# An eighth accumulation bank for C22 in a seven-product matmul kernel, side products moved to four banks between seven-product pairs

## The chip, the cores and the metric

The kernel runs on one core of a Trainium2 chip. The metric is the device time of one execution in microseconds (us); a median over several runs is given. The engines are PE (TensorE, matmuls), DVE (VectorE), ACT (ScalarE), POOL (GpSimd) and SP (SyncE); POOL and SP only issue DMAs here, apart from a few small powers on POOL.

## The reference

A trunk of two layers over 256 tokens of width 4096, all in float32. The two large products of a layer, into 11,264 columns and back from 4096 to 4096, make nearly all of the work.

```
for l in range(DEPTH):                       # DEPTH = 2
    h = rmsnorm(x, norm_w[l])
    proj = h @ w_in[l]                       # (256 x 4096) @ (4096 x 11264)
    aq, ak, av, ag, rq, rk, rv, rg = split(proj)
    a_out = silu(ag) * gqa_attention(rope(norm(aq)), rope(norm(ak)), av)     # 16 heads, 4 for keys
    r_out = silu(rg) * rmsnorm(bidirectional_retention(rope(rq), rope(rk), rv))   # 8 heads
    x = x + concat([a_out, r_out]) @ w_out[l]   # (256 x 4096) @ (4096 x 4096)
return rmsnorm(x, final_norm)
```

## The kernel before

**Blocks.** Each projection is cut into blocks of 2 x 512 columns: 11 blocks for `w_in`, 4 for `w_out`, so that the two layers have four *stages* with 11, 4, 11 and 4 blocks. One block computes a 2 x 2 array of outputs C11, C12, C21, C22 (two halves of 128 tokens by two halves of 512 columns). The 32 row tiles of the contraction are taken as 16 *pairs* (`NP`), each a 2 x 2 by 2 x 2 product.

**Precision.** A float32 operand is split into a rounded high part and the rest as a low part (`whi`, `wlo` for weights, `x8h`, `x8l`, `x7h`, `x7l` for activations). One *product* is three matmuls of 128 x 128 by 128 x 512: high x high and low x high of the operand with the weights' high part (L1472), and high x the weights' low part (L1482). In the very first block pairs 0 and 1 (`NATIVE`) are taken unsplit in one slower matmul each (L1466).

**Seven or eight products.** A pair costs eight products. Pairs in the seven-product set (`SEVEN`, with pair 10 added in stages 1, 2 and 3 by `MORE`) use Winograd's form with seven: sums of weights and sums of activations are formed first (`xf` in `split_pair`, `wsum` in `Weights.begin`), and the seven products go to seven banks M1 to M7 of the accumulator memory (each bank holds 128 x 512 numbers). So that eight-product pairs can share these seven banks, they don't accumulate C22 in a bank of its own: one bank (M3) takes a *difference operand*, x of the one half minus x of the other, and M5 takes both halves' rest:

```
EIGHT_PRODUCTS: ("M3", 1, 2, PAGE_A, 1), ("M5", 1, 1, PAGE_A, 1), ("M4", 0, 1, PAGE_A, 0), ("M2", 0, 0, PAGE_A, 0), ...
```

The second index 2 is the difference, which `split_pair` makes for each eight-product pair (`x3`, shown as `x` in the profile), and which the first stage makes later, in `third`. Only the first block of all (`PLAIN`) has an eighth bank, which has the tag `ps`, and there `PLAIN_PRODUCTS` is used.

**Pages.** The weights of a pair come in two pages of 128 x 1024 (A, B); a seven-product pair has two more for the sums (T, U). A page is loaded by SP into one of 5 raw buffers, ACT rounds it (`whi`), DVE subtracts (`wlo`), and PE uses it; 5 such pages are in the ring. For some pages (`FAR_PAIRS`, `FAR_OUT`) the low part is made without DVE: ACT writes minus the high part (`flo`), and POOL adds the weights to it by a DMA that reads them a second time (L521).

**Between blocks.** As soon as a bank has its last product, `combine` adds it into the block's output pages `ca`, `cb` (DVE, at M1 ACT). All products of the last pair are sorted by bank (`LAST_ORDER`), so that the banks come free one after the other before the next block starts with them.

**Side products.** Attention and retention need 576 small matmuls of their own (L988 to L990). They share the eighth bank, `ps`: `take_bank` waits until it is free, `free_bank` returns it. Their steps are *tasks* and *lanes* (Python generators) that a planner (`tick`, `advance`, `running`) places between the products: it keeps a modelled time of PE, DVE and ACT, lets a task step run only where the next pages still come in time (`Weights.room`, with `STEP_V`, `STEP_S`, `MARGIN`), and counts *pages* of working memory (`PAGES` = 9). The order that it finds at build time is the order of the instructions on the chip.

**End.** In the last block, products of bank M4 with the pairs in `DELAYED` (5) come last, so that the other half's output is finished beside them (`last_combine`).

Of the kernel before, what the change touches and what calls it, by code (L numbers as in the profile page):

```python
# [17 lines left out]
P = 128  # L18
# [17 lines left out]
PAGES = 9  # L36
# [5 lines left out]
STEP_V = 0.8  # L42
STEP_S = 1.5

V_FIXED = 0.1
S_FIXED = 0.12

MM = {512: 0.2268, 256: 0.1177}
PASS = 0.3

LANDING = 9.5
STORE = 7.0
FETCH = 13.0
FAR_LANDING = 11.0
MARGIN = 0.8

RUSH = 0.5
# [3 lines left out]
ADD_AHEAD = 0.5  # L61

NEED = {"ak": 4, "ag": 4, "rk": 5, "rg": 4}

PE_REST = 1.5

TIGHT_A = 2
TIGHT_B = 9

AT_ONCE = 2  # L70
# [19 lines left out]
PLAIN = 1  # L90

DEFER = (0,)

FAR_PAIRS = (2, 8, 11, 14)

FAR_OUT = (5, 14)
# [17 lines left out]
def constants():  # L114
# [60 lines left out]

SEVENS = [tuple(sorted(SEVEN + MORE)) if _s in MORE_IN else SEVEN for _s in range(2 * DEPTH)]
EVER = sorted(SEVEN + MORE)
EIGHTS = [_p for _p in range(NP) if _p not in EVER]

GROUPS = [[tuple(range(_a, _b)) for _a, _b in zip(_s, _s[1:] + (NP,))] for _s in SEVENS]  # L180


def pages_of(group, first=False):

    order, one = [], group[:1]
    rest = group[1:]
# [12 lines left out]
def is_far(stage, p, k):  # L199

    return k == PAGE_B and p in (FAR_OUT if stage % 2 else FAR_PAIRS)


def slots_of(group, stage, first=False, plain=False):

    for _p, _k in pages_of(group, first):
        if _p in SEVENS[stage] and not (first and _p in NATIVE):
            yield [(_b, _p, (ALL, _a), _k, _h) for _b, _a, _pg, _h in SEVEN_PRODUCTS if _pg == _k]
        else:
            eight = PLAIN_PRODUCTS if plain else EIGHT_PRODUCTS  # L210
            yield [(_b, _p, (_i, _a), _k, _h) for _b, _i, _a, _pg, _h in eight if _pg == _k]
# [3 lines left out]
LAST_ORDER = ("M3", "M5", "M4", "M2")  # L215
FINAL_ORDER = ("M5", "M2", "M3", "M4")
PLAIN_ORDER = ("M3", "M8", "M4", "M2")
# [7 lines left out]
TOGETHER = 3  # L225
# [3 lines left out]
TURNS = "02"  # L229

ABREAST = False
# [46 lines left out]
def hybrid_encoder(  # L278
# [136 lines left out]
    class Weights:  # L415


        def __init__(self):
            self.pages = []
            for l in range(DEPTH):  # L420
                for w, n in ((w_in, N_IN), (w_out, N_OUT2)):
                    for b in range(n):
                        stage = 2 * l + (w is w_out)
                        for g in GROUPS[stage]:
                            start = (l, b) == (0, 0) and w is w_in
                            for slot in slots_of(g, stage, start):
# [5 lines left out]
                                    start and (g in GROUPS[0][:2] or one.whole)  # L432
# [164 lines left out]
    def dead_room():  # L597

        if not rooms:
            e, o = len(EIGHTS), len(EVER)  # L600
            kinds = {
                "x3": ("x3", e, [P, 2, 2, P], "p k s t -> p (k s t)"),
# [5 lines left out]
            for p in range(NP):  # L608
                if p not in EIGHTS:
                    rooms.extend(kinds[v] for v in ("x7h", "x7l"))  # L610
                else:
                    rooms.extend(kinds[v] for v in ("x3", "x8h", "x8l")[: 3 if p in EIGHTS[2:] and p not in DELAYED else 1])
# [20 lines left out]
    def split_pair(p, v, whole, stage):  # L633
# [39 lines left out]
        else:  # L673
            if p in EIGHTS:
                hi = t(ap, [P, 2, SEQ], "x8h", len(EIGHTS), F32R)
                lo = t(ap, [P, 2, SEQ], "x8l", len(EIGHTS), F32R)
                g = t(ap, [P, 2, 2, P], "x3", len(EIGHTS), F32R)
                g = [g[:, k] for k in range(2)]
            else:
                both = [t(ap, [P, 7, P], v, len(EVER), F32R) for v in ("x7h", "x7l")]  # L680
                hi, lo = (v[:, 0:4, :].rearrange("p (i m) t -> p i (m t)", m=MT) for v in both)
                g = [v[:, 4:6, :] for v in both]
            g4 = [tokens(v) for v in g]
# [10 lines left out]
            if stage in DEFER:  # L694
                thirds.append(Lane(None))
                thirds[-1].steps = third(p, hi, lo, g, thirds[-1])
                thirds[-1].pair, thirds[-1].at_work = p, False
            else:
# [8 lines left out]
        operand[p] = (hi, lo) if p in SEVENS[stage] else (hi, lo, g)  # L707
# [3 lines left out]
    def third(p, hi, lo, g, one):  # L711

        while held[0] + pledged() >= PAGES:
            yield
        one.at_work = True
        v = page([P, 2, 2, P], "x3f")
        d, e = v[:, 0], v[:, 1]
        for u, v in ((d, hi), (e, lo)):
            ve.tensor_sub(u, f32(v)[:, :, :P], f32(v)[:, :, P:])
        ve.tensor_add(d, d, e)  # L720
        yield
        ac.copy(g[0], d)
        yield
        ve.tensor_sub(g[1], d, f32(g[0]))
        drop()
        operand_at[p] = ve.until + PASS
        yield

    as_it_comes, thirds = {}, []

    def third_step():
        one = thirds[0]
        if not one.at_work and held[0] + pledged() >= PAGES:
            advance()
            return
        one.step()
        if one.done:
            thirds.pop(0)
# [92 lines left out]
    bank = [False, 0.0]  # L831
# [9 lines left out]
    def free_bank():  # L841
        bank[0], bank[1] = False, max(ve.until, ac.until) + BANK_REST

    class Lane:
        def __init__(self, steps, heavy=True, need=0, own=0, owner=None):
# [41 lines left out]
    def running():  # L887
# [3 lines left out]
        if rest and len(one) < AT_ONCE:  # L891
            need = held[0] + rest[0].need - rest[0].own + sum(max(0, w.need - w.own) for w in one)
            if need <= PAGES:
                one.append(rest[0])
# [946 lines left out]
```

## Time and profile before

| | |
|---|---|
| median of 3 runs | 2619.73 us (2616.75 to 2621.66) |
| profiled execution | 2620.23 us |
| its span, first to last instruction | 2618.4 us |
| granted clock of PE | 0.998 |
| DVE operations on `wlo<-wraw,whi` | 853, 929.5 us |
| ACT casts `whi<-wraw` | 853, 808.8 us |
| DMA moved | 660.34 MB, mean 252 GB/s |

The page gives the busy time of each engine, its share of the span and the number of instructions, then the clock granted to PE in 40 slices (9 is full), then the chain of work that ended last. In a row of a timeline the first number is the start and the second the duration of one, both in us; in a group the numbers behind the bar are busy us and mean ns of one, then the idle time before them and what ended it. A row of the waits has the total, the number of waits and the longest. A row of a window has its length, then busy us (and instructions) of PE, PEld (weight loads of PE), DVE, ACT and POOL, then the clock, the DMA share and GB/s.

### The profile page before, as it was taken

The page shows a single profiled execution, that of the slowest core. Times are in us where ns is not written, and L with a number is a line of the kernel's source. Part 1 is how long each engine was busy: PE and PEld are TensorE (multiplying, and loading weights), DVE is VectorE, ACT ScalarE, POOL GpSimd, SP SyncE. Part 2 cuts the span into 40 slices and gives each one's busy share as a digit, 9 for nine tenths or more (in the row PEclk, how much of TensorE's full clock was granted, in tenths as well). Part 3 has the DMA queues.
Part 4 walks back from the last instruction along what each step waited for, and adds up shares of the span by engine and source line. Part 5 has one row for each costly group of instructions (what it writes and reads, how often), then busy time and mean ns, then how long its engine had stood idle before and what let it go on. Part 6 is the DMA issues. An engine that isn't in the chain of part 4 may idle for free.

```text
span 2618.4 us, 34300 instructions
## 1 busy us (share of the span) xinstructions
PE 2595.2 (99%) x11596; PEld 2142.3 (82%) x11596; DVE 2257.9 (86%) x2786; ACT 1774.0 (68%) x2552; POOL 325.7 (12%) x464
## 2 busy tenths in 40 slices
PE   9999999999999999999999999999999999999998
PEld 7778888888888888888878888888888888788886
DVE  7898887888878899887998989988898798998787
ACT  8767676656655787555886767676566567876554
POOL 0012221201101100111111112221011011000000
PEclk9999999999999999999999999999999999999999
DMA  8888888878777776887788888878787777767785
GB/s 308 290 256 273 278 266 268 266 253 258 221 228 243 242 243 212 262 270 236 273 249 255 274 268 266 285 251 275 250 256 224 237 245 247 225 211 244 241 252 186
DMA packets 194497, 660.34 MB, mean 252 GB/s; under 512 B 23440, under 2 KB 30096, under 8 KB 194320
## 3 DMA queue, kind: packets, MB, share of 16 engines
q1 hardware_dynamic: 147760, 521.27, 57.0%
q0 software_dynamic: 46560, 136.87, 21.8%
q8 instruction: 91, 1.49, 0.2%
q14 instruction: 86, 0.70, 0.1%
HBM read 614.01 MB, written 44.04 MB: 251 GB/s over the span
## 4 chain that ended last, share of the span: by engine, by line
PE 92%; DMA 3%; DVE 2%; ACT 2%; issue 1%; SPq 0%; DVEq 0%; POOLq 0%; POOL 0%; ACTq 0%
PE M L1472 59%; PE M L1482 29%; DMA wraw<-in_w_in 2%; DVE wlo L263 1%; PE ps L989 1%; PE ps L988 1%; PE ps L990 1%; ACT whi L263 1%; DMA flo<-in_w_in 0%; PE M L1466 0%; DMA ca<-in_x 0%; DVE wsum L263 0%; ACT to L263 0%; PE ps L1472 0%; DMA fhi<-in_w_in 0%
## 5 line engine op out<-in xcount | busy, mean ns | idle before, releaser
L263 ACT CAST whi<-wraw 128x1024 fp32r<-128x1024 f32 (+1 forms) x853 | 808.8, 960 | 476.3 <-PE M L1472 284.1
L263 DVE TENSOR_TENSOR wlo<-wraw,whi 128x1024 fp32r<-128x1024 f32 (+1 forms) x853 | 929.5, 1107 | 155.5 <-ACT whi L263 146.6
L1472 PE MATMUL M<-whi,x8h 128*128 128x512 f32 x1467 | 572.6, 390 | 0.8 <-DVE ca L263 0.8
L1472 PE MATMUL M<-whi,x8l 128*128 128x512 f32 x1467 | 571.5, 390 | 0.0
L1482 PE MATMUL M<-wlo,x8h 128*128 128x512 f32 x1467 | 505.0, 389 | 0.0
L1472 PE MATMUL M<-whi,x7h 128*128 128x512 f32 x1262 | 491.6, 390 | 2.3 <-DVE cb L263 1.3
L1472 PE MATMUL M<-whi,x7l 128*128 128x512 f32 x1262 | 491.4, 389 | 0.0
L263 ACT CAST whi<-wsum 128x1024 fp32r<-128x1024 f32 x336 | 352.8, 1050 | 185.7 <-PE M L1472 130.2
L263 DVE TENSOR_TENSOR wlo<-wsum,whi 128x1024 fp32r<-128x1024 f32 x336 | 409.5, 1219 | 70.6 <-ACT whi L263 63.0
L1482 PE MATMUL M<-wlo,x7h 128*128 128x512 f32 x1262 | 414.1, 390 | 0.7 <-DVE wlo L263 0.2
L1472 PEld LDWEIGHTS M<-whi,x8h 128*128 128x128 f32 x1467 | 275.8, 188 | 60.7 <-DVE ca L263 3.2
L1472 PEld LDWEIGHTS M<-whi,x8l 128*128 128x128 f32 x1467 | 275.8, 188 | 57.2 <-issue 0.2
L1482 PEld LDWEIGHTS M<-wlo,x8h 128*128 128x128 f32 x1467 | 275.7, 188 | 57.1
L1472 PE MATMUL M<-whi,x 128*128 128x512 f32 x960 | 296.2, 390 | 1.1 <-ACT whi L263 1.1
L1482 PEld LDWEIGHTS M<-wlo,x7h 128*128 128x128 f32 x1262 | 236.6, 188 | 52.9 <-DVE wlo L263 3.9
L1472 PEld LDWEIGHTS M<-whi,x7h 128*128 128x128 f32 x1262 | 237.1, 188 | 51.3 <-DVE cb L263 1.6
L1472 PEld LDWEIGHTS M<-whi,x7l 128*128 128x128 f32 x1262 | 237.0, 188 | 48.2
L263 DVE TENSOR_TENSOR wsum<-wraw 128x1024 f32<-128x1024 f32 x168 | 204.2, 1216 | 29.4 <-DMA wraw<-in_w_in 26.1
L1472 PEld LDWEIGHTS M<-whi,x 128*128 128x128 f32 x960 | 180.1, 188 | 38.8 <-ACT whi L263 1.5
L1482 PE MATMUL M<-wlo,x 128*128 128x512 f32 x480 | 187.2, 390 | 0.4 <-DVE wlo L263 0.4
L521 POOL DMA_DIRECT2D flo<-in_w_in x87 | 79.4, 913 | 825.3 <-ACT flo L263 812.8
L263 ACT CAST fhi<-wraw 128x1024 fp32r<-128x1024 f32 (+1 forms) x103 | 107.9, 1048 | 88.8 <-PE M L1472 88.6
(298 smaller groups left out, 2873.5 us busy)
## 6 DMA issues: line engine op xcount, KB each, us to landing
wraw<-in_w_in SPq DMA_DIRECT2D x700, 512.0 KB, 5.0
wraw<-in_w_out SPq DMA_DIRECT2D x256, 512.0 KB, 4.6
flo<-in_w_in POOLq DMA_DIRECT2D x87, 512.0 KB, 7.9
full<-next_dram POOLq DMA_DIRECT2D x18, 512.0 KB, 8.2
p_dram<-room POOLq DMA_DIRECT2D x64, 128.0 KB, 4.7
pT<-p_dram POOLq DMA_DIRECT2D x16, 512.0 KB, 7.8
flo<-in_w_out POOLq DMA_DIRECT2D x15, 512.0 KB, 7.6
next_dram<-room POOLq DMA_DIRECT2D x40, 128.0 KB, 5.3
```

Of the source, the lines that this page charges most:

```text
L263: return call(out, *args, **kwargs)
L521: nc.gpsimd.dma_start(g.lo[h], g.src[0][:, h, :], accum_op=ALU.add)
L988: nc.tensor.matmul(out, a[0], b[0], start=start, stop=False)
L989: nc.tensor.matmul(out, a[0], b[1], start=False, stop=False)
L990: nc.tensor.matmul(out, a[1], b[0], start=False, stop=stop)
L1472: nc.tensor.matmul(acc[name], a[i], g.hi[h], start=m == first[name] and not i, stop=False)
L1482: nc.tensor.matmul(acc[name], a, g.lo[h], start=False, stop=m == final[name])
```

## The change

- An eighth bank, M8, takes C22 in all blocks. Eight-product pairs use the list that was `PLAIN_PRODUCTS`. The difference operand, its tile and `third` are gone.
- `SEVENS` names the seven-product pairs of each stage. Each stage has 5; pair 0 is in none, so a block opens and, past the last of them, closes with eight-product pairs, which don't use M1, M5, M6 and M7.
- Side products take any of these four banks (`SHARED`), in the *window* from the end of a block's last seven-product pair to the start of the next block's first. `take_bank`, `free_bank`, `near` and gates on tasks see to that. In the first block of an output projection (`hurried`) all side work has to be placed before the first seven-product pair.
- Attention's scores and values become two tasks; retention's weights are a gated lane. Tasks start in any order that fits (`startable`).
- `PAGES` is 13 instead of 9. The constants of the planner change, `TOGETHER` is 4 (so many products of a page are issued with their high parts first), and fewer pages are read twice (`FARS`).
- Four pairs instead of five are delayed at the end.

```diff
-PAGES = 9
+PAGES = 13
...
-STEP_V = 0.8
-STEP_S = 1.5
+STEP_V = 1.6
+STEP_S = 0.7
...
-SEVEN = (0, 3, 6, 9, 12)
-
-MORE = (10,)
-
-MORE_IN = (1, 2, 3)
-
-DELAYED = tuple([_p for _p in range(NP) if _p not in SEVEN + MORE][-5:])
+SEVENS = ((3, 5, 7, 9, 11), (5, 7, 9, 10, 11), (3, 5, 7, 9, 11), (5, 7, 10, 11, 12))
+
+EVER = sorted(set(_p for _s in SEVENS for _p in _s))
+EIGHTS = [_p for _p in range(NP) if _p not in EVER]
+
+DELAYED = tuple(EIGHTS[-4:])
...
-FAR_PAIRS = (2, 8, 11, 14)
-
-FAR_OUT = (5, 14)
+FARS = ((2, 12), (1, 8), (12,), (15,))
...
 EIGHT_PRODUCTS = [
-    ("M3", 1, 2, PAGE_A, 1),
-    ("M5", 1, 1, PAGE_A, 1),
-    ("M4", 0, 1, PAGE_A, 0),
-    ("M2", 0, 0, PAGE_A, 0),
-    ("M4", 1, 1, PAGE_B, 1),
-    ("M5", 0, 1, PAGE_B, 0),
-    ("M3", 0, 2, PAGE_B, 0),
-    ("M2", 1, 0, PAGE_B, 1),
-]
-
-PLAIN_PRODUCTS = [
     ("M3", 1, 0, PAGE_A, 1),
     ("M8", 1, 1, PAGE_A, 1),
...
+SHARED = ("M1", "M5", "M7", "M6")
...
-LAST_ORDER = ("M3", "M5", "M4", "M2")
-FINAL_ORDER = ("M5", "M2", "M3", "M4")
+LAST_ORDER = ("M3", "M8", "M4", "M2")
+FINAL_ORDER = ("M8", "M2", "M3", "M4")
...
-TOGETHER = 3
+TOGETHER = 4
...
-            if stage in DEFER:
-                thirds.append(Lane(None))
-                thirds[-1].steps = third(p, hi, lo, g, thirds[-1])
-                thirds[-1].pair, thirds[-1].at_work = p, False
-            else:
-                ve.tensor_sub(x0, x0, x1)
-                yield
-                ac.copy(g4[0], x0)
-                yield
-                ve.tensor_sub(g4[1], x0, f32(g4[0]))
...
     def take_bank():
 
-        while bank[0] or now.t < bank[1]:
-            yield
-        bank[0] = True
+        while not (window[1] and any(v <= now.t for v in spare.values())):
+            yield
+        name = min(spare, key=lambda v: spare[v])
+        del spare[name]
+        taken[name] = None
         yield "PE"
-        return t(pm, [P, NB], "ps")
+        taken[name] = t(pm, [P, NB], name)
+        return taken[name]
...
             if n == first[name]:
-                acc[name] = t(pm, [P, NB], "ps" if name == "M8" else name)
+                if name in SHARED:
+                    if name == SHARED[0] and hurried:
+                        while users:
+                            advance()
+                    window[1] = False
+                    while name in taken:
+                        advance()
+                    now.wait(spare.pop(name, 0.0))
+                acc[name] = t(pm, [P, NB], name)
...
         if bank == "M6":
             ve.tensor_add(cb[:, 0, :], ca[:, 0, :], acc["M6"])
             ve.tensor_add(ca[:, 1, :], cb[:, 0, :], acc["M7"])
-            if "M8" in acc:
-                combine("M5 and M6", acc, c)
+            ve.tensor_add(cb[:, 1, :], ca[:, 1, :], acc["M5"])
+            ve.tensor_add(cb[:, 0, :], cb[:, 0, :], acc["M5"])
+            for v in SHARED:
+                spare[v] = ve.until + BANK_REST
+            window[:2] = [99, True]
         elif bank == "M8":
             ve.tensor_add(cb[:, 1, :], cb[:, 1, :], acc["M8"])
-            free_bank()
```

More of the change, by code (lines that the diff above doesn't have):

```diff
@@ L174, with pages_of @@
 ]
[L176 to L186, printed above, removed]
+GROUPS = [
+    ([tuple(range(_s[0]))] if _s[0] else []) + [tuple(range(_a, _b)) for _a, _b in zip(_s, _s[1:] + (NP,))] for _s in SEVENS
+]
+SHARED = ("M1", "M5", "M7", "M6")
+def pages_of(group, stage, first=False):
+    n = 1 if group[0] in SEVENS[stage] else 0
+    order, one, rest = [], group[:n], group[n:]
     if first:
@@ L431, in __init__ @@
                                 one.far = is_far(stage, one.pair, one.kind) and not (
-                                    start and (g in GROUPS[0][:2] or one.whole)
+                                    start and (one.pair < 6 or one.whole)
                                 )
@@ L706, in split_pair @@
         version[p] += 1
-        operand[p] = (hi, lo) if p in SEVENS[stage] else (hi, lo, g)
+        operand[p] = (hi, lo)
         operand_at[p] = max(ve.until, ac.until) + PASS
         yield
-    def third(p, hi, lo, g, one):
-        while held[0] + pledged() >= PAGES:
-            yield
[L715 to L738, printed above, removed]
+    as_it_comes = {}
     def split_operand(c, stage, rest=0.0):
@@ L879, in pledged, with startable @@
     def pledged():
-        return sum(max(0, v.need - v.own) for i, v in enumerate(tasks) if v.begun or not i)
+        return want[0] + sum(max(0, v.need - v.own) for v in tasks if v.begun)
+    def startable():
+        free = PAGES - held[0] - pledged()
+        return next((v for v in tasks if not v.begun and v.need - v.own <= free and (not v.gate or v.gate())), None)
     def pledge(n):
@@ L1407, in begin_product @@
                     need(p, phase)
-                    while not plain and any(v.pair == p for v in thirds):
-                        third_step()
                     now.wait(operand_at[p])
```

184 lines of the change are left out of this document (102 added, 82 removed).

## The prediction

> **What bounds the kernel now.** I read the page first (shares and slices, then the chain that ended last), then the timeline of PE, then the waits of PE, then the engines' busy time in the stretches where PE waits.
>
> ```profile
> span 2618.4 us, 34300 instructions
> ...
> PE 2595.2 (99%) x11596; PEld 2142.3 (82%) x11596; DVE 2257.9 (86%) x2786; ACT 1774.0 (68%) x2552; POOL 325.7 (12%) x464
> ...
> PEclk9999999999999999999999999999999999999999
> ...
> PE 92%; DMA 3%; DVE 2%; ACT 2%; issue 1%; SPq 0%; DVEq 0%; POOLq 0%; POOL 0%; ACTq 0%
> ```
>
> PE is busy for 99% of the span at full clock and makes 92% of the chain. "Busy" may hide slack, because the ends of matmuls are modelled, so I count matmuls at their pitch (start to start) instead. The timeline of PE gives the first matmuls of the projection, the last whole-width one of the opening, a run of twelve 256-wide side products with the matmul behind it, and the last matmul of all. One row of the chain in order of time gives six 512-wide matmuls with nothing between them.
>
> ```profile
> 6.15 1.10 PE L1466 MATMUL M<-fhi,full 128*128 128x512 f32 x2 [0.61 <-DMA fhi<-in_w_in]
> ...
> 19.56 0.80 PE L1472 MATMUL M<-whi,x8h 128*128 128x512 f32 x1
> ...
> 662.03 0.28 PE L988 MATMUL ps<-vh,wTh 128*128 128x256 f32 x1
> ...
> 663.46 0.63 PE L1482 MATMUL M<-wlo,x8h 128*128 128x512 f32 x2
> ...
> 2605.81 0.39 PE L1482 MATMUL M<-x7l,x8h 128*128 128x512 f32 x1
> ```
>
> ```profile
> 97.26 1.36 PE M L1472 x6
> ```
>
> The pitch of a 512-wide matmul is 1.36/6 = 0.2267 us, that of a 256-wide one (663.46 - 662.03)/12 = 0.119 us. The products before, counted from the block lists, are 10,968 matmuls of 512 columns in the blocks, 96 of 512 and 480 of 256 columns in the side products (attention and retention), and 16 whole-precision ones at the start, which take 19.56 - 6.15 = 13.4 us. So PE needs 11,064 x 0.2267 + 480 x 0.119 + 13.4 = 2579 us between 6.15 and 2605.81, which is 2599.7 us. **20.6 us is all that PE loses on the way.** Outside lie the first 6.15 us, the 12.6 us after the last matmul, and 1.8 us around the span: the profiled execution took 2620.23 us. The median of the runs shown is 0.5 below it.
>
> Where the 20.6 us lie is shown by three stretches, each with matmuls (x), busy time of PE, PEld, DVE and ACT, and clock:
>
> ```profile
> 85.00:190.00 105.00, 99.99 (x431) 79.92 (x431) 93.22 (x146) 66.36 (x104) 14.44 (x18) 1.00 0.82 259
> 1285.00:1375.00 90.00, 89.16 (x388) 72.02 (x388) 84.32 (x119) 77.37 (x134) 6.91 (x8) 1.00 0.77 240
> 2230.00:2280.00 50.00, 47.99 (x207) 38.58 (x206) 47.99 (x71) 39.32 (x59) 3.74 (x5) 0.97 0.79 242
> ```
>
> 431 matmuls at 0.2267 are 97.7 us, so the first loses 7.3; the second loses 90 - 88.0 = 2.0; the third holds 12 of the 256-wide ones and loses 50 - 44.2 - 1.4 = 4.4. That is 13.7 of 20.6 us in 245 us, and these are the start and the changes from one projection to the next, where DVE is busy 89, 94 and 96% of the time against 86% in the span. The waits that the trace names there:
>
> ```profile
> PE M L1472 <- ACT whi L263: 2.1, 2, 1.1
> PE ps L988 <- DVE D L263: 1.8, 1, 1.8
> PE M L1482 <- DMA flo<-in_w_in: 1.3, 1, 1.3
> PE M L1472 <- DVE cb L263: 1.3, 1, 1.3
> ```
>
> **The change part by part.**
>
> *Products.* A pair of row tiles costs 8 products of three matmuls, or 7 where it is in the seven-product set. The sets of the four projections have 5, 6, 6, 6 pairs before and 5 in each after. The second, third and fourth have 4, 11 and 4 blocks, so 19 products are added. In the very first block pairs 0 and 1 are whole-precision and don't count: before, 4 of the set are left there, after, 5; one product goes. Net 18 products, 54 matmuls, and the order of the two kernels on PE has 11,580 and 11,634. 54 x 0.2267 = **+12.2 us**. All of it is on the path, since nothing covers PE. The other six banks' products keep their number: M8 takes the product that went to M5 through the difference operand.
>
> *Vector work.* It lies beside PE and costs nothing unless it comes late; the sum tells how much cover there is. Rows with durations:
>
> ```profile
> L263 DVE TENSOR_TENSOR wlo<-wraw,whi 128x1024 fp32r<-128x1024 f32 x676 | 817.4, 1218 | 143.0 <-ACT whi L263 134.4 <-PE M L1472 6.6
> L263 DVE TENSOR_TENSOR wlo<-wsum,whi 128x1024 fp32r<-128x1024 f32 x336 | 409.5, 1219 | 70.6 <-ACT whi L263 63.0 <-PE M L1472 7.1
> L263 DVE TENSOR_TENSOR wsum<-wraw 128x1024 f32<-128x1024 f32 x168 | 204.2, 1216 | 29.4 <-DMA wraw<-in_w_in 26.1 <-DMA wraw<-in_w_out 3.1
> L263 DVE TENSOR_TENSOR wlo<-wraw,whi 128x512 fp32r<-128x512 f32 x177 | 120.8, 683 | 12.5 <-ACT whi L263 12.3
> L263 DVE TENSOR_TENSOR wsum<-wsum,wraw 128x512 f32<-128x512 f32 x168 | 116.3, 692 | 5.8
> L263 DVE TENSOR_TENSOR cb<-cb,M 128x512 f32<-128x512 f32 x61 | 41.4, 680 | 10.6 <-PE M L1482 10.6
> L263 DVE TENSOR_TENSOR full<-full 128x256 f32<-128x256 f32 x21 | 8.9, 425 | 0.7
> L263 DVE TENSOR_TENSOR x<-full,x 128x256 fp32r<-128x256 f32 x21 | 8.8, 417 | 0.0
> L263 ACT ACTIVATE flo<-fhi 128x1024 fp32r<-128x1024 f32 x102 | 108.3, 1062 | 3.2
> ```
>
> By the order, whole low parts of pages grow by 79 x 1.218 = 96 us (59 of them pages no longer read twice), those of sums fall by 36 x 1.219 = 44, half ones by 20 x 0.683 = 14, the sums themselves by 18 x (1.216 + 2 x 0.69) = 47; the difference operand falls in 30 places at 0.425 + 0.417 and in 11 at four times 0.42, together 44; the adds of banks grow from 210 to 240, 30 x 0.68 = 20. DVE: -33 us of 2258, so about 85% instead of 86%. ACT loses 59 x 2.1 on pages read twice against some 40 casts more elsewhere: about -100 us. The cover grows a little, no more.
>
> *Pages read twice.* They fall from 102 to 43:
>
> ```profile
> flo<-in_w_in POOLq DMA_DIRECT2D x87, 512.0 KB, 7.9
> ...
> flo<-in_w_out POOLq DMA_DIRECT2D x15, 512.0 KB, 7.6
> ```
>
> 59 x 0.5 MB is 31 of 660 MB, and 59 issues leave POOL's queue. Of PE's waits only the 1.3 us for flo at 86 us is such a page, in the first block, where 3 such pages become 1. Gain between 0 and 1.5; I take 0.8, the middle, since one such page stays there.
>
> *Side products.* Before, they share one bank and are strewn over the block; after, they use M1, M5, M6, M7 only from the last seven-product pair of a block to the first of the next. Their number stays 576, so their PE time stays. What one bank can cost is shown at 2255 us of the timeline, by rows of DVE and the row of PE that waited:
>
> ```profile
> 2254.99 1.22 DVE L263 TENSOR_TENSOR wlo<-wraw,whi 128x1024 fp32r<-128x1024 f32 x1
> ...
> 2256.13 0.42 DVE L263 TENSOR_TENSOR x<-full,x 128x256 fp32r<-128x256 f32 x1
> 2256.46 0.68 DVE L263 SCALAR_TENSOR_TENSOR D<-ps,D 128x512 f32<-128x512 f32 x1
> ...
> 2257.20 0.39 PE L988 MATMUL ps<-rkqh 128*128 128x256 f32 x1 [1.75 <-DVE D L263]
> ```
>
> PE waits until DVE, behind a page and a difference operand, has emptied the bank. The next product now takes another bank, and the difference is gone, so this wait goes.
>
> *Bank turnover between blocks.* The new place for waits. All four of M3, M8, M4, M2 are filled to the end of a block, and the next block opens with them. By the lists, M3 and M4 have 18 matmuls between their last and their next first use, M8 and M2 have 14: 3.2 us. DVE's add takes 0.68 and the matmul's end another 0.39, so it must start within 2.1 us. I added DVE's instructions in the order of the changed kernel at the durations above and took off 0.2267 for each matmul that the order puts between: what stands ahead of a bank's add is 0.6 us in the middle and 2.4 at most (near 174 and 1300 us). The same sum on the kernel before gives up to 5.9 near 165 us and 3.9 near 2250, which is where the waits for cb and D stand. So I cost it at 0.3 us for each of the few places above 2.1, 1 us in all; 0 and 29 x 1 us bound it.
>
> *Pages, limits, order.* Four pages more, and the constants of the planner, issue nothing; they move steps, and what that does is in the sum just given. At the end the last bank takes 8 products after M3's instead of 10, so its add comes 1.4 us sooner behind the first half's output.
>
> ```profile
> 2606.24 0.69 DVE L263 TENSOR_TENSOR ca<-ca,M 128x512 f32<-128x512 f32 x1 [1.62 <-PE M L1482]
> ...
> 2607.02 0.60 ACT L263 ACTIVATE ps<-ca 128x512 f32<-128x512 f32 x1 [3.05 <-DVE ca L263]
> ```
>
> Both engines idle longer than 1.4 us there: nothing, at most 0.5.
>
> **The sum.** 2620.2 + 12.2 for the matmuls. Of the 20.6 us lost I let go: 0.8 (flo), 4.4 - 1.0 = 3.4 of the last change of projection (one bank, difference), and half of the rest of the start and the second change, (7.3 + 2.0 - 1.3)/2 = 4.0, as what stands ahead of a bank's add there falls from 5.9 to 2.4 us; add 1.0 for bank turnover. That is 7.2 less, and 20.6 becomes 13.4. 2620.2 + 12.2 - 7.2 = 2625.2; 0.5 less for the median and 1.7, a quarter of the 6.9 us lost outside the three stretches, for waits there that end: **2623 us**, 0.1% above the median. A measurement of this kernel can tell 0.2% from no change, 2614.5 to 2625.0.
>
> **Rivals.** (1) *The waits stay.* They may be late transfers and casts, not DVE: ACT whi is the greatest of PE's waits, and the start stays full of loads. Then 2620.2 + 12.2 - 0.5 = 2632, slower. For it: the cover grows by one point only. Against: 3.1 us of the quoted waits name DVE's D and cb. (2) *Turnover of four banks at once.* If DVE is more than 2.1 us late at most block ends, 29 ends at 0.7 to 1 us give 2623 + 20 to 29, 2643 to 2652, slower. It decides from that 2.1 us on. A long wait costs twice, as the stretch after the wait at 2255 us shows, with the clock as the seventh figure:
>
> ```profile
> 2257.00:2262.00 5.00, 4.80 (x17) 3.94 (x18) 4.73 (x6) 4.32 (x11) 0.00 (x0) 0.66 0.94 339
> ```
>
> A wait of 1.75 us was followed by a clock of 0.66 over 5 us, 1.7 us more. [...] (4) *All waits go:* 2620.2 + 12.2 - 20.6 - 0.5 = 2611 if nothing at all is lost, and 2614 to 2617 with 3 to 6 us that stay.
>
> **How the numbers follow.** Forecast 0.50 (2617 to 2626), waits stay 0.31 (2626 to 2635), turnover 0.10, clock 0.02, all waits go 0.07, half of that under 2614.5. The range 2617 to 2635 leaves out about 0.19. Faster 0.03; same 0.46 of the forecast and 0.04 of the last, 0.50; slower 0.47.
>
> **What would show it.** 11,650 matmul records (the whole-precision ones count double) at 0.2267. A loss, counted as above, near 12 us. No wait of a side product for D, x3 or its bank; DVE under 86%. Wrong if PE waits for cb or ca at many block ends, or if the loss stays near 20 us. The sum itself can't be wrong by much downwards, since 2611 is its floor.

## The result, and the profile after

The kernel with the change takes **2624.76 us** (median of 13 runs, 2623.52 to 2626.36), the kernel before 2619.73 us beside it (13 runs, 2616.75 to 2623.61): ratio 1.0019, 95% interval 1.0010 to 1.0028. It is slower by 5 us, 0.19%. The interval lies above 1, so the 5 us are real, though they are under the 0.2% that the prediction took as the limit of no change. The forecast was 2623.0.

The page after (span, busy time of the engines, clock in 40 slices, chain that ended last):

```profile
span 2622.3 us, 33965 instructions
...
PE 2604.2 (99%) x11650; PEld 2151.5 (82%) x11650; DVE 2231.7 (85%) x2666; ACT 1684.6 (64%) x2411; POOL 274.6 (10%) x413
...
PEclk9999999999999999999999999999999999999999
...
PE 94%; DVE 3%; issue 1%; ACT 1%; DMA 1%; SPq 0%; DVEq 0%; POOLq 0%; POOL 0%; ACTq 0%
```

PE has the 11,650 records that were counted; DVE lost one point of its share, ACT four and POOL two. None of this says what PE waited for. So the prediction's sum is made again, from the first and the last matmul and the end of the opening in the timeline of PE:

```profile
5.65 2.31 PE L1455 MATMUL M<-fhi,full 128*128 128x512 f32 x4
8.71 1.98 PE L1455 MATMUL M<-flo,full 128*128 128x512 f32 x4 [0.74 <-DMA flo<-in_w_in]
...
20.43 0.79 PE L1461 MATMUL M<-whi,x8h 128*128 128x512 f32 x1
...
2609.64 0.39 PE L1471 MATMUL M<-x8l,x8h 128*128 128x512 f32 x1
```

PE needs 11,118 x 0.2267 + 480 x 0.119 + the opening's 14.8 = 2592.4 us, and 2609.64 - 5.65 = 2604.0 us passed: **11.6 us are lost**, against 20.9 before (20.6 in the prediction, which rounded). The spans differ by 3.9 us: +12.2 for 54 matmuls, +1.4 for the opening, -9.3 for what is lost on the way, -0.4 at the ends. The medians differ by 1.1 us more than that; the profiled execution after is 0.7 us faster than its median, and a trace of one execution can't show where the others take longer.

The waits of PE after (total, number, longest):

```profile
PE M L1471 <- DVE wlo L248: 2.4, 5, 1.3
PE M L1693 <- DVE junk L248: 1.1, 1, 1.1
PE M L1461 <- ACT whi L248: 1.0, 1, 1.0
PE M L1455 <- DMA flo<-in_w_in: 0.7, 1, 0.7
PE M L1461 <- DVE cb L248: 0.2, 1, 0.2
```

No side product (L943 to L945) is in it, and no difference operand. The same three stretches as before, and a fourth one, first of the kernel after, then (last row) the fourth one of the kernel before:

```profile
85.00:190.00 105.00, 104.84 (x461) 86.05 (x460) 90.24 (x125) 74.41 (x125) 12.52 (x17) 1.00 0.83 276
1285.00:1375.00 90.00, 89.77 (x395) 73.69 (x394) 84.18 (x112) 75.61 (x132) 4.34 (x5) 1.00 0.69 229
2230.00:2280.00 50.00, 50.00 (x233) 41.76 (x232) 39.53 (x51) 37.00 (x59) 3.25 (x5) 1.00 0.68 228
...
2330.00:2345.00 15.00, 13.42 (x57) 10.20 (x56) 14.93 (x20) 10.01 (x12) 0.00 (x0) 1.00 0.49 167
```

```profile
2330.00:2345.00 15.00, 15.00 (x68) 12.43 (x67) 14.15 (x20) 14.42 (x26) 0.00 (x0) 1.00 0.61 206
```

461 matmuls in the first stretch leave 0.5 us instead of 7.3, 395 in the second 0.5 instead of 2.0, and in the third PE is busy throughout instead of losing 4.4. So 13.7 us became 1.0. In the fourth, 57 matmuls at 0.2267 are 12.9 us: 2.1 are lost where nothing was lost before, with DVE busy for 14.93 of 15 us.

### The profile page after: what moved, and what is told of

Same layout as the page of the kernel before. It is cut to its first block, busy times and chain, and to the rows that moved or that the text cites. A ratio compares the mean times of both kernels' runs of the same rounds, so it can differ in the third digit from the quotient of the medians.

```text
span 2622.3 us, 33965 instructions
## 1 busy us (share of the span) xinstructions
PE 2604.2 (99%) x11650; PEld 2151.5 (82%) x11650; DVE 2231.7 (85%) x2666; ACT 1684.6 (64%) x2411; POOL 274.6 (10%) x413
## 2 busy tenths in 40 slices
DMA packets 187151, 633.58 MB, mean 242 GB/s; under 512 B 22624, under 2 KB 29280, under 8 KB 186976
## 4 chain that ended last, share of the span: by engine, by line
PE 94%; DVE 3%; issue 1%; ACT 1%; DMA 1%; SPq 0%; DVEq 0%; POOLq 0%; POOL 0%; ACTq 0%
PE M L1461 60%; PE M L1471 30%; DVE wlo L248 1%; PE M L945 1%; PE M L944 1%; PE M L943 1%; DMA wraw<-in_w_in 1%; DVE wsum L248 1%; PE M L1455 0%; ACT whi L248 0%; ACT ca L248 0%; DMA flo<-in_w_in 0%; DVE ca L248 0%; DVE x7l L248 0%; DVE ls L248 0%
## 5 line engine op out<-in xcount | busy, mean ns | idle before, releaser
L248 ACT CAST whi<-wraw 128x1024 fp32r<-128x1024 f32 (+1 forms) x912 | 878.5, 978 | 529.8 <-PE M L1461 346.2
L248 DVE TENSOR_TENSOR wlo<-wraw,whi 128x1024 fp32r<-128x1024 f32 (+1 forms) x912 | 1007.5, 1127 | 156.3 <-ACT whi L248 147.6
L1461 PE MATMUL M<-whi,x8h 128*128 128x512 f32 x2042 | 795.7, 390 | 0.2 <-DVE cb L248 0.2
L1461 PE MATMUL M<-whi,x8l 128*128 128x512 f32 x2042 | 795.2, 389 | 0.0
L1471 PE MATMUL M<-wlo,x8h 128*128 128x512 f32 x2042 | 586.3, 389 | 0.0
L1461 PEld LDWEIGHTS M<-whi,x8h 128*128 128x128 f32 x2042 | 383.4, 188 | 80.8 <-DVE cb L248 1.3
L1461 PEld LDWEIGHTS M<-whi,x8l 128*128 128x128 f32 x2042 | 383.4, 188 | 79.0 <-DVE x7l L248 0.2
L1471 PEld LDWEIGHTS M<-wlo,x8h 128*128 128x128 f32 x2042 | 382.1, 188 | 78.8
L248 DVE TENSOR_TENSOR wsum<-wsum,wraw 128x512 f32<-128x512 f32 x150 | 103.8, 692 | 5.2
L248 DVE TENSOR_TENSOR wsum<-wraw,wsum 128x512 f32<-128x512 f32 x150 | 102.4, 683 | 0.1
```

The lines of the kernel that those rows point to most:

```text
L248: return call(out, *args, **kwargs)
L1461: nc.tensor.matmul(acc[name], a[i], g.hi[h], start=m == first[name] and not i, stop=False)
L1471: nc.tensor.matmul(acc[name], a, g.lo[h], start=False, stop=m == final[name])
```

## Experiments

All kernels against the kernel before on the same chip; "lost" is the sum above, made for the profiled run of each. Where a loss is given for a part of the span, the gaps between matmuls beyond their pitch are added up there.

| kernel | median us | ratio (95%) | 512-wide | lost us |
|---|---|---|---|---|
| before | 2619.73 | 1 | 11,064 | 20.9 |
| after | 2624.76 | 1.0019 (1.0010 to 1.0028) | 11,118 | 11.6 |
| before, five pairs | 2628.78 | 1.0034 (1.0022 to 1.0046) | 11,121 | 18.3 |
| before, no difference operand | 2617.89 | 0.9996 (0.9987 to 1.0005) | 11,064 | 21.1 |
| before, fewer pages twice | 2651.86 | 1.0125 (1.0111 to 1.0139) | 11,064 | 51.2 |
| after, pairs spread | 2619.84 | 1.0000 (0.9991 to 1.0009) | 11,118 | 8.9 |
| after, six pairs | 2674.73 | 1.0209 (1.0195 to 1.0223) | 11,061 | 75.7 |
| after, alternating pairs | 2660.04 | 1.0159 (1.0145 to 1.0173) | 11,118 | 47.4 |
| after, one bank | 2785.72 | 1.0639 (1.0625 to 1.0654) | 11,118 | 173.3 |
| after, two banks | 2624.90 | 1.0019 (1.0010 to 1.0028) | 11,118 | 12.0 |
| after, more pages twice | 2640.30 | 1.0081 (1.0067 to 1.0094) | 11,118 | 27.3 |
| spread, four pairs twice | 2623.54 | 1.0013 (1.0004 to 1.0022) | 11,118 | 7.1 |
| spread, six in outputs | 2634.10 | 1.0056 (1.0043 to 1.0068) | 11,094 | 27.2 |
| the same pairs, fewer pages twice, other constants | 2632.49 | 1.0050 (1.0036 to 1.0063) | 11,094 | 25.3 |

### The count alone: the kernel before with five pairs

```diff
-MORE_IN = (1, 2, 3)
+MORE_IN = ()
```

> The kernel before with five seven-product pairs in all four stages, nothing else changed: 57 matmuls more. Theory (count times pitch, less what DVE's relief ends of the waits): 57 x 0.2267 = 12.9 us; each of the 19 pairs that turn from seven to eight products takes some 4.5 us off DVE, so of the 20.6 us lost some go: 2625 to 2631. Rival (the waits are late transfers and casts that DVE's load has no part in): 12.9 us flat, 2632.6, with the loss counted over PE's records still near 20 us.

It takes 2628.78 us, 8.9 more than the kernel before beside it (2619.86). 57 matmuls more are 12.9 us, and 2.6 us fewer are lost, so the time is within the theory's range, but most of the loss stays: 18.3 us, 8.3 of it in the stretch from 85 to 190 us, where the kernel before lost 7.6 (both from the gaps between matmuls). DVE falls to 83%, under the 85% of the kernel after. So the load of DVE as a mean does not explain why the change ends the waits. What is gone here is the wait of a side product for D at 2255 us (the stretch from 2230 to 2280 us loses 0.7 instead of 4.7), though the single bank and the difference operand are both still there.

### The difference operand alone

```diff
-    ("M3", 1, 2, PAGE_A, 1),
+    ("M3", 1, 0, PAGE_A, 1),
...
-    ("M3", 0, 2, PAGE_B, 0),
+    ("M3", 0, 0, PAGE_B, 0),
...
-                ve.tensor_sub(x0, x0, x1)
-                yield
-                ac.copy(g4[0], x0)
-                yield
-                ve.tensor_sub(g4[1], x0, f32(g4[0]))
```

The operand isn't made, and M3 takes x of the one half in its place, so C22 is another sum; products and banks keep their number.

> The kernel before without the difference operand: its subtraction, cast and low part are not made, and M3 takes the first half's own operand in its place, so the output is not the reference's. The number of matmuls stays 11,580. Theory (the difference is vector work that comes late at the start and at the changes of projection): 3 to 7 us of the 20.6 us lost go, 2613 to 2617. Rival (late transfers and casts): within 1.5 us of the kernel before.

2617.89 us, no change (0.9996), with 21.1 us lost. The waits of PE in it:

```profile
PE M L1472 <- DMA flo<-in_w_in: 3.5, 2, 2.5
PE M L1472 <- DVE wlo L263: 2.3, 4, 0.9
PE M L1462 <- ACT whi L263: 2.2, 3, 1.3
PE ps L978 <- DVE D L263: 1.8, 1, 1.8
```

37 us of DVE are gone (2221.3 instead of 2257.9 us) and, in sum, nothing of the loss. It isn't made up of the same waits, though. The waits for cb and ca of the kernel before, 2.1 us, are gone, and so are the two for whi at 129 and 133 us; waits for flo (2.46 us at 160 us, with a clock of 0.66 over the 5 us behind it, and 1.0 us at 1372 us) and for low parts have come in their place. The side product that waited 1.8 us for D behind a difference operand still waits 1.8 us without it, so the operand wasn't what kept it. The single bank is left as a cause, but not as one that is enough by itself: the kernel before with five pairs has one bank too, and no such wait.

### Pairs spread

```diff
-SEVENS = ((3, 5, 7, 9, 11), (5, 7, 9, 10, 11), (3, 5, 7, 9, 11), (5, 7, 10, 11, 12))
+SEVENS = ((3, 5, 7, 9, 11), (5, 7, 9, 11, 12), (3, 5, 7, 9, 11), (5, 7, 9, 11, 12))
```

> The changed kernel with the seven-product pairs 5, 7, 9, 11, 12 in the second and fourth stage, so that no three of them follow each other; the matmuls stay 11,634. Theory (three in a row need more of DVE than PE's time gives, and PE waits for low parts there): the waits of x7h products on wlo in these two stages, some 4 us, go: 2620 to 2622. Rival (these waits come from making the operands at the change of projection): no change, 2624 to 2626.

2619.84 us, 4.9 less than the kernel after with the same matmuls, and level with the kernel before. Why three seven-product pairs in a row cost something can be read from the groups of DVE in the kernel after (busy us, mean ns):

```profile
L248 DVE TENSOR_TENSOR wlo<-wraw,whi 128x1024 fp32r<-128x1024 f32 x755 | 906.2, 1220 | 147.7 <-ACT whi L248 144.9
L248 DVE TENSOR_TENSOR wlo<-wsum,whi 128x1024 fp32r<-128x1024 f32 x300 | 365.9, 1220 | 42.6 <-ACT whi L248 42.4
L248 DVE TENSOR_TENSOR wsum<-wraw 128x1024 f32<-128x1024 f32 x150 | 182.5, 1216 | 29.9 <-DMA wraw<-in_w_out 14.0 <-DMA wraw<-in_w_in 9.2 <-issue 6.1
L248 DVE TENSOR_TENSOR wlo<-wraw,whi 128x512 fp32r<-128x512 f32 x157 | 107.5, 685 | 8.6 <-PE M L1471 6.0 <-ACT whi L248 2.6
L248 DVE TENSOR_TENSOR wsum<-wsum,wraw 128x512 f32<-128x512 f32 x150 | 103.8, 692 | 5.2
L248 DVE TENSOR_TENSOR wsum<-wraw,wsum 128x512 f32<-128x512 f32 x150 | 102.4, 683 | 0.1
```

A seven-product pair needs, on DVE, one whole low part (1.22), the sums (1.22 + 0.69 + 0.68), two low parts of sums (2.44) and half a page (0.69): 6.94 us. PE is through with it in 21 x 0.2267 = 4.76 us. An eight-product pair needs 2.44 us on DVE and 5.44 on PE. Counting these steps alone, DVE falls 2.2 us behind on the one kind and gains 3.0 on the other; three in a row put it 6.5 us behind, and the ring of pages has to hold that much. In the kernel after they stand in pairs 9 to 11 and 10 to 12 of the output projections, and four of its five waits for low parts lie in three of the eight blocks there. The fourth stretch and the waits of the kernel with pairs spread:

```profile
2330.00:2345.00 15.00, 14.71 (x66) 11.80 (x65) 14.97 (x16) 11.30 (x13) 0.00 (x0) 1.00 0.67 226
```

```profile
PE M L1471 <- DVE wlo L248: 1.1, 3, 0.6
```

66 matmuls instead of 57, and waits for low parts of 1.1 us instead of 2.4. The profiled runs differ by 3.2 us, 2.7 of it in the loss, and 1.7 of that lies between 2300 and 2400 us. The rest of the 4.9 between the medians isn't located. The theory had 4 us of waits for low parts; there were 2.4, and 1.3 of them went.

### Six pairs, and alternating pairs

```diff
+SEVENS = ((3, 5, 7, 9, 11), (5, 7, 9, 10, 11, 12), (3, 5, 7, 9, 10, 11), (5, 7, 9, 10, 11, 12))
```

> The changed kernel with six seven-product pairs in the second, third and fourth stage (5,7,9,10,11,12; 3,5,7,9,10,11; 5,7,9,10,11,12): 57 matmuls fewer. Theory (matmuls cost their pitch, and waits come where DVE has more than its time): 2624.8 - 12.9 = 2611.9 plus up to 1 us of new waits on low parts in each of the 19 blocks, 2613 to 2631, with the waits in the runs of three and four pairs. Rival (count alone): 2612.

2674.73 us: 57 matmuls fewer are 12.9 us won, and 64 more are lost. The first two of its waits:

```profile
PE M L1471 <- DVE wlo L248: 22.8, 42, 1.5
PE M L1461 <- DVE x7l L248: 11.4, 2, 7.7
```

42 waits for low parts, with four such pairs in a row in the output projections (8.7 us behind) and three in the second layer's input projection. The size was far above what either theory gave.

```diff
+SEVENS = ((4, 6, 8, 10, 12),) * 4
...
+FARS = ((2, 13), (1, 9), (13,), (15,))
```

> The changed kernel with the seven-product pairs 4, 6, 8, 10, 12 in all stages, never two in a row; three of the pages read twice move to eight-product pairs beside them, and the matmuls stay 11,634. Theory (low parts are late where seven-product pairs follow each other): no wait on a low part over 0.5 us; the loss falls below that of the spread version (8.9), 2617 to 2620. Rival (what is left of the loss isn't from the order of the pairs): 2619 to 2621.

2660.04 us, a miss for both: operands of the next projection come late, x7l above all.

```profile
PE M L1461 <- DVE x7l L248: 14.4, 6, 5.2
PE M L1461 <- ACT whi L248: 5.8, 5, 1.9
```

Moving the pairs moves everything that is planned around them, and the planner's constants were not chosen anew for it. Waits for low parts are 9 here, 3.1 us in all and 0.6 at most, though no two such pairs follow each other. So a row of such pairs is not the only thing that makes low parts late.

### One bank, two banks

```diff
-            for v in SHARED:
+            for v in SHARED[-1:]:
                 spare[v] = ve.until + BANK_REST
```

> The changed kernel with one bank, M6, lent to side products instead of four; its matmuls and windows stay. Theory (with one bank a side product waits until DVE or ACT has emptied it, and the window of some 48 products, 33 us, gets tight): waits of side products on what empties the bank come back, 2 to 25 us, 2627 to 2650. Rival (the windows are long enough for one bank at a time, four gain nothing): 2623 to 2626, like the changed kernel.

2785.72 us, 173 lost, part of it by slower matmuls (the granted clock is 0.971 over the span). Two stretches of it, a hundred us each (the clock is the seventh figure), lie at the change from an input to an output projection and at the same place of the second layer:

```profile
1000.00:1100.00 100.00, 60.62 (x239) 48.79 (x238) 56.15 (x93) 61.24 (x125) 10.27 (x16) 0.72 0.29 92
...
2400.00:2500.00 100.00, 64.85 (x248) 51.79 (x249) 63.51 (x104) 66.51 (x133) 4.44 (x7) 0.70 0.23 79
```

What happens in them, from the timeline of PE, DVE and ACT:

```profile
1052.33 0.58 PE L943 MATMUL M<-vh,wTh 128*128 128x256 f32 x1 [6.80 <-ACT vh L248]
1052.92 4.95 ACT L248 COPY ca<-room 32x256 f32<-32x256 f32 x12
...
1055.44 0.41 PE L945 MATMUL M<-vh,wTl 128*128 128x256 f32 x1
1057.89 0.38 ACT L248 ACTIVATE junk<-M 128x256 bf16<-128x256 f32 x1
...
1060.10 0.88 DVE L248 SCALAR_TENSOR_TENSOR ca<-M,rst,ca 128x256 f32<-128x256 f32 x2 [0.90 <-POOL rst L394]
1061.03 0.58 PE L943 MATMUL M<-vh,wTh 128*128 128x256 f32 x1 [5.17 <-DVE ca L248]
```

Twelve side products, then 12 copies on ACT, a square, a power on POOL and an add on DVE until the bank is free: PE stands 5.2 us, and the bank is what it waits for: it has nothing else to do, as the block may not go on to its first seven-product pair. The kernel before has one bank too, with side products anywhere in a block, and there one wait of 1.8 us is for that bank. So it is with the window that one bank is too few. The kernel with two:

```diff
-            for v in SHARED[-1:]:
+            for v in SHARED[-2:]:
```

> The kernel after with side products in two of the four shared banks, M7 and M6; nothing else is changed. With one bank the time was 2785.7 us and 173 us were lost between the first and the last matmul, against 11.6 with four. Theory (what one bank lacks is a second one to fill while DVE or ACT empties the first; a product's bank is emptied about as fast as the next is filled): two banks do as well as four, loss 9 to 15 us, 2622 to 2628 us. Rival (each bank counts, because DVE comes to empty a bank only after a page, 1.2 us, and its own queue): the loss falls with the number of banks, and two keep a third of the 162 us, some 50 us, 2660 to 2690 us, with waits of side products for D and ca.

2624.90 us, 12.0 lost: as with four. The theory held: a second bank to fill while the first is emptied is all that the window needs, and the third and fourth bring nothing that can be measured.

### Pages read twice

```diff
-FARS = ((2, 12), (1, 8), (12,), (15,))
+FARS = ((2, 8, 12, 14), (1, 8), (2, 8, 12, 14), (6, 15))
```

> The changed kernel with as many pages read twice as the kernel before (103 issues of flo instead of 44); the matmuls stay. Theory after the run without the difference operand (the waits of the first 200 us and the changes of projection come from transfers, and the changed kernel lost them because it moves 31 MB less): the loss counted over PE's records goes up from 11.6 by 4 to 8 us, most of it under 200 us, 2628 to 2633. Rival (other things in the changed order ended the waits; DVE has 60 pages less to make, so it may even gain): 2621 to 2625.

2640.30 us, above both ranges: 15.7 us more are lost, 10.8 of them past 1300 us, although DVE is busy less (82%). In the first 200 us it loses 5.1 instead of 1.7 us. The other direction, on the kernel before:

```diff
-FAR_PAIRS = (2, 8, 11, 14)
+FAR_PAIRS = (2, 11)
```

> The kernel before with 59 pages read twice instead of 103: pairs 8 and 14 are taken off that list in the first and third stage. Its matmuls stay 11,580. Theory (transfers make the early waits): the loss counted over PE's records falls from 20.9 by 3 to 8 us, 2612 to 2617. Rival (they relieve DVE of 44 pages, 54 us, in a kernel whose DVE is full, so that low parts come later): the loss rises, 2620 to 2630.

2651.86 us, again above both ranges. The first 200 us lose 5.3 instead of 7.7, and the wait for flo is gone; everything behind is worse (7.8 us for wlo, 5.5 for pr, 5.2 for ca). The loss rises, as the rival said, but by 30 us, with 49 us more work on DVE (2306.8 us, 87%). Each of these two edits changes the order of all that follows, and with it more than the page reads; the runs don't separate the two. A third run came closer to keeping the order: pairs spread, and only the first stage's pages changed.

```diff
-FARS = ((2, 12), (1, 8), (12,), (15,))
+FARS = ((2, 8, 12, 14), (1, 8), (12,), (15,))
```

> The third kernel of this study (seven-product pairs spread, 2619.8 us) with four pairs of the first layer's input projection read twice, as before, instead of two: (2, 8, 12, 14) for (2, 12); the order of the rest hardly moves. Its loss in the first 200 us was 2.1 us, that of the kernel before 7.7. Theory (pages read twice are what ends about half of the early waits): 2 to 4 us more are lost in the first 200 us, with a wait of PE for flo of over 1 us, and little elsewhere, 2621 to 2624 us. Rival (the early waits came from the order and the planner's constants, and pages read twice are hidden by the other loads): the first 200 us lose 2 us as they did, no wait for flo over 0.7 us, 2619 to 2621 us.

The timeline of PE has one wait of the kind that was expected, at the place where the kernel before has it (86.6 us):

```profile
88.75 1.20 PE L1471 MATMUL M<-flo,x8h 128*128 128x512 f32 x4 [1.26 <-DMA flo<-in_w_in]
```

But the first 200 us lose 2.7 instead of 2.1 us, not 2 to 4 more, since other small waits are shorter there. The median of 2623.54 us is 3.7 above that of pairs spread, and its ten runs lie between 2619.09 and 2627.20; the profiled one is the fastest, so the trace can't show what the others lose. So: pages read twice make the wait at 87 us, 1.3 us; what else they cost is open.

### A sixth pair in the output projections

The pairs of the kernel with pairs spread, with pair 6 added in both output projections, and the pages read twice and five of the planner's constants chosen for it:

```diff
+SEVENS = ((3, 5, 7, 9, 11), (5, 6, 7, 9, 11, 12), (3, 5, 7, 9, 11), (5, 6, 7, 9, 11, 12))
+FARS = ((2, 12), (1, 8), (1, 13), (8, 15))
+STEP_V = 2.0
+EARLY = 1.0
+PE_REST = 1.2
+TIGHT_A = 1
+LATE = 15
```

> The kernel after with a sixth seven-product pair in both output projections, pairs (5, 6, 7, 9, 11, 12), the input projections spread as in the third kernel, and the planner tuned for it (three constants and the pages read twice). 8 products fewer, 24 matmuls, 5.4 us. Theory (the time is matmuls times pitch plus a loss that a fitting order keeps near 9 us): 2619.8 - 5.4 = 2614.4 us, range 2612 to 2618, faster than both kernels. Rival (three seven-product pairs in a row, 5, 6, 7, bring waits for low parts again, eight blocks at 1 to 3 us): loss 17 to 33 us, 2622 to 2638 us.

2634.10 us: missed, with a loss in the rival's range but not in its place. The second layer's input projection, whose pairs didn't change, first with pairs spread, then in this kernel:

```profile
1300.00:2250.00 950.00, 949.86 (x4275) 788.65 (x4274) 829.46 (x975) 603.59 (x856) 106.22 (x163) 1.00 0.73 237
```

```profile
1300.00:2250.00 950.00, 943.88 (x4238) 780.25 (x4237) 816.43 (x975) 621.56 (x894) 118.16 (x178) 1.00 0.75 243
```

37 matmuls fewer in 950 us; counted by their widths (48 fewer of 512 columns, 12 more of 256) 9.6 us more are lost here, 11.5 instead of 2.0, and DVE is even less busy. The pairs of this stage are not in a row. What changed for it are the pages read twice (1 and 13 instead of 12), the constants and the order that follows from them; which of them costs the time isn't shown. This kernel also shows bank turnover past its deadline, at the change from the first input projection to the output projection (timeline of PE and DVE):

```profile
974.85 0.69 DVE L248 TENSOR_TENSOR cb<-cb,M 128x512 f32<-128x512 f32 x1
...
976.38 1.22 DVE L248 TENSOR_TENSOR wTl<-D,wTh 128x1024 fp32r<-128x1024 f32 x1
977.52 0.68 DVE L248 TENSOR_TENSOR cb<-cb,M 128x512 f32<-128x512 f32 x1
...
978.25 0.50 PE L1461 MATMUL M<-whi,x8h 128*128 128x512 f32 x1 [1.87 <-DVE cb L248]
```

Between the adds of two banks DVE has four small sums for operands and a low part of 1.22 us, 2.1 us in all, and PE waits 1.87 us for the second bank. There are two more such waits, near 1315 us: three in all, 4.0 us.

The next kernel has the same pairs, but of the constants above only `TIGHT_A`; the others are those of the kernel after, with four of its own:

```diff
+FARS = ((2, 12), (2,), (), (15,))
+LANDING = 10.0
+MARGIN = 0.8
+TIGHT_A = 1
+HOLD = 8
+AT_ONCE = 6
```

> As the kernel with six pairs in the output projections, but with fewer pages read twice (one pair in the first output projection, none in the second layer's input projection) and other planner constants. DVE makes some 12 low parts more, 15 us of 2232. Theory (what counts is the order, not whether DVE or a second read makes the low part, with DVE at 85%): within 3 us of its sister, 2612 to 2618 us. Rival (pages read twice relieve DVE where three seven-product pairs stand in a row): 4 to 10 us slower than its sister, waits for wlo after 2300 us.

2632.49 us, within 3 us of its sister, as the theory said, but both are 14 to 16 us above their ranges. Pages and constants were changed at once, so that the two agree doesn't show that the page reads are without effect. Here losses lie in the output projections too (13.8 us past 2250 and from 960 to 1300 us), with waits for banks (cb) and for low parts, seven of these after 2300 us as the rival said:

```profile
PE M L1471 <- DVE wlo L248: 5.1, 12, 0.8
PE M L1461 <- DVE cb L248: 4.3, 5, 1.9
```

No run of this study is measurably faster than the kernel before. The nearest is the kernel with pairs spread, level with it while making 54 matmuls more.

## Why the prediction was right, and where it was not

- **Products: right.** 54 matmuls at 0.2267 us. In the table the loss is what the count leaves over, so the table can't test this price by itself. Two things do: in the first stretch of the kernel after, where PE hardly waits, 461 matmuls take 105 us, 0.2278 each; and the 57 matmuls of the kernel before with five pairs made the span 10.5 us longer, 12.9 less the 2.6 that it lost less.
- **The total loss: right in size, by luck, and wrong in place.** Forecast 13.4 - 1.7 = 11.7 us, measured 11.6. But the three stretches were to fall from 13.7 to 5.5 us and fell to 1.0, and everything else was to fall from 6.9 to 6.2 (1.7 less for waits that end, 1.0 more for bank turnover) and rose to 10.6. Two errors of about 4.5 us cancel. The term that was sized by a guess, "half of the rest of the start and the second change" (4.0 us), measured 7.0.
- **Vector work: right in size, wrong as a cause.** DVE went from 2257.9 to 2231.7 us (-26, forecast -33), to 85% as said. The step that failed is "what stands ahead of a bank's add there falls" as the reason for half of the gain at the start. Without the difference operand the waits for cb and ca do go, but others of the same size take their place (21.1 us lost), and at 83% DVE 18.3 us are still lost. That the waits at the start end in the kernel after is shown; why isn't. Several things came with the eighth bank at once: pair 0 left the seven-product set, so that a block opens with an eight-product pair, `TOGETHER` and `PAGES` grew, and the planner's constants changed. None of these was tried by itself on the kernel before.
- **Three pairs in a row: missing from the prediction.** It listed the pairs of each stage for the count alone. The rows it quoted gave DVE's 6.9 us a pair against PE's 4.8, and with them a reason to expect the wait that ends at 2333 us. The price of such a row isn't fixed by these rates: its waits come in three of eight blocks, and alternating pairs have waits for low parts too.
- **Side products: right in the number, with the reason not shown.** The wait of 1.75 us at 2255 us is gone, and none took its place. The difference operand was not its cause. That further banks ended it isn't shown either, since it is also gone in the kernel before with five pairs and in the one with fewer pages read twice, both with one bank (which costs the latter 5.5 us elsewhere, in six waits of side products for `pr`). What the banks are needed for is the window, and there two do what four do.
- **Bank turnover: right.** Forecast 1.0 us between 0 and 29; one wait for cb, 0.2 us. With the sixth pair three such waits (4.0 us, 1.87 the longest) and in its sister five (4.3 us) came as the prediction had described them, so the margin is not wide.
- **Pages read twice: about right.** 0.8 forecast; the wait at 86 us was 1.3 and comes back as 1.3 with the pages. DMA moved 633.58 MB instead of 660.34, 27 less and not 31, because `kv` is now read in 16 transfers of 512 KB instead of 8.
- **The opening: missing.** It took 14.8 us instead of 13.4, of which 0.7 is a wait for flo. Over the kernels of the table it is 13.4 to 14.1 us in the old order and 14.0 to 14.9 in the new, so part of this is the run.
- **Rivals.** That the waits stay (2632) comes nearest to the kernel before with five pairs, 2628.8, where most of them do; in the kernel after they don't. Turnover of four banks (2643 to 2652) is refuted by one wait of 0.2 us. The chance of 0.02 for the clock stands for a dip at every block end, which neither kernel shows: taken in windows of 5 us, the clock before is under 1.00 only in the two around and behind the wait of 1.75 us (0.84 and 0.82, 2255 to 2265 us) up to 2605 us, and after in none up to 2610 us. The granted clock is 0.998 over the span as before. But PE waits at the block ends only once in the kernel after, for 0.2 us, so what a wait at every block end would do to the clock isn't shown. That all waits go fails by 11.6 us.

## What to carry to other kernels

Where PE is 99% busy, predict by counting matmuls at their pitch and by listing, one by one, the waits that remain; the count came out exactly here, and the waits are where the error was. Look at how fast the feeding engine works per kind of step, not at its mean load: a kind that needs 6.9 us where PE needs 4.8 can make PE wait when it comes three times in a row (2.4 us for low parts here, 1.1 with the pairs spread), whatever the mean of 85% says. When shared work is squeezed into a window, the bank that was enough while it lay spread out may not be (173 us lost with one here), but a second one may be all that it takes (12.0 lost, as with four). And a wait that is gone after a change is not yet one that the change ended: look whether it goes in a kernel that lacks the part to which you put it down.

## What the runs showed of the hardware

A wait of PE of 1.90 us was paid for twice in the kernel with more pages read twice. The timeline of PE and the windows around that wait, which was for flo:

```profile
89.61 1.77 PE L1471 MATMUL M<-flo,x8h 128*128 128x512 f32 x4 [1.90 <-DMA flo<-in_w_in]
91.17 0.63 PE L1461 MATMUL M<-whi,x8h 128*128 128x512 f32 x1
91.60 0.63 PE L1461 MATMUL M<-whi,x8l 128*128 128x512 f32 x1
```

```profile
90.00:92.00 2.00, 2.00 (x6) 1.56 (x5) 1.07 (x1) 2.00 (x5) 0.00 (x0) 0.50 1.02 414
92.00:95.00 3.00, 3.00 (x12) 2.38 (x11) 0.85 (x2) 2.97 (x7) 0.55 (x1) 0.77 1.04 403
```

After 1.90 us without work the pitch is 0.43 us, with a clock of 0.50 over 2 us and 0.77 over the next 3: 2 x 0.50 + 3 x 0.23 = 1.7 us more. The wait of 1.26 us at the same place, in the kernel with four pairs twice, was followed by a clock of 1.00, and so was the wait of 1.27 us that ends at 2333 us in the kernel after. In these traces length alone doesn't decide. The wait of 1.75 us in the prediction had a dip behind it, and a wait without one is longer than all of these: 2.66 us in the kernel before with five pairs (timeline of PE, then the three us behind the wait, with a clock of 1.00).

```profile
130.06 0.74 PE L1472 MATMUL M<-whi,x 128*128 128x512 f32 x2 [2.66 <-ACT whi L263]
```

```profile
130.00:133.00 3.00, 2.94 (x12) 2.17 (x12) 2.96 (x9) 2.91 (x12) 0.00 (x0) 1.00 0.21 56
```

The wait of 1.87 us at 978 us of the kernel with a sixth pair had no dip either (1.00 from 979 to 982 us). Its sister has one of the same length at 977 us, with another of 0.86 us just ahead of it, and the clock behind it dips:

```profile
977.00:980.00 3.00, 3.00 (x10) 2.38 (x10) 3.00 (x4) 0.92 (x2) 0.00 (x0) 0.68 0.19 56
```

In the kernel before, the waits of 1.0 to 1.3 us at 86, 129, 133 and 186 us had none: the clock is 1.00 from 86 to 91, from 126 to 134 and from 182 to 190 us. So of the waits looked at here those of 1.0 to 1.3 us had no dip behind them, and of the longer ones those of 1.75, 1.90 and 2.46 us had one, as the last of 1.87 us had, while the first of 1.87 us and the one of 2.66 us had none. What decides isn't shown.
